# Reading spilled tiles back ahead of time: the first down chunk's forms, the last block's parts and the gate rows move from GpSimd's queue to the weights' queue

## The chip, the cores and the metric

One core of a Trainium2 chip runs the whole kernel. The metric is device time in microseconds (us) of one execution; 0.3% of it is 6.6 us. TensorE (PE) multiplies, VectorE (DVE) and ScalarE (ACT) do everything elementwise, GpSimd (POOL) and SyncE (SP) here only issue transfers: SP's queue loads weights, POOL's queue carries the traffic to and from scratch memory in DRAM.

## The reference, cut to what matters

```python
x = x + gate_m * rms_norm(o, g_post_mix)                  # the mixer's residual, 512 tokens x 2048
h = rms_norm(x, g_pre_ffn) * (1.0 + scale_f) + shift_f
f = (silu(h @ w_ffn_gate) * (h @ w_ffn_up)) @ w_ffn_down  # 2048 -> 5632 -> 2048
x = x + gate_f * rms_norm(f, g_post_ffn)                  # gate_f: a part of silu(c) @ w_ada + b_ada
```

Everything is float32. The kernel splits each operand into a rounded high part and the rest (hi, lo) and makes three matmuls of each product (`mm3`, L214 to L216).

## The kernel before, in words

**Up phase.** The 5632 FFN columns are cut into 22 blocks of 256 (`NBLK`). A block is worked in two halves `s` of the contraction. Of each half the gate and the up weights come as one load of 1 MB each (`raw_of`, L912) on SP's queue into four `wr` buffers. Seven products in the manner of Strassen (`q1`, `q2`, `q5`, `r7`, `r6`, `q4`, `r3`) replace eight; each takes sums of weights (`vadd`, L924), split by ACT (L906) and DVE (L907) into `wh` buffers, against a *form* of the activations (`a11`, `s1`, ...) that lies in SBUF. A half is 168 matmuls of 128x256.

**Spill.** All 128x512 tiles share one pool of 73 buffers (`t2`, tiles named `t`). After each pair of blocks, `pair_forms` makes the seven forms of the pair's result, and `spill_parts` stores hi and lo of each to DRAM (`gd`, L948, POOL's queue). The last pair (blocks 20, 21) stores no forms, only hi and lo of its four results (`gd[-1]`, eight tiles).

**Down phase.** Ten of the eleven pairs are consumed in five chunks `c_` of two pairs. A chunk makes, for each half `p` of the output columns, seven products of 24 matmuls of 128x512. At the first use of a form in a chunk, `back` (L1024) loads its four 256 KB tiles from DRAM on POOL's queue, 28 loads in a chunk. The down weights are loads of 1 MB on SP's queue (`w_fd`). ACT (L1042) copies a product to its accumulator in the first chunk, DVE adds it (L924) in the others; after the last chunk DVE combines the accumulators (L924, L838).

**Tail.** The last pair is multiplied plainly. `gate_rows(1, ...)` turns the column of FFN gates into four row tiles: two DVE operations on `ggcol`, a transpose by PE (L254), a copy by DVE (L256), a store to DRAM (`gg`, L257), and four loads that spread each quarter over 128 partitions (L260), the last two steps on POOL's queue. Eight `back` loads (`gl`) follow them there. Four loads of 1 MB (`w_fl`, SP's queue) are split into `t` tiles by ACT (L1082) and DVE (`minus`, L838). Then follow four token tiles times four column groups of 12 matmuls, each with an add (L1098), a square, a multiply by the gate row (L1101), and per token tile a norm, the residual (L1107) and the store of `y`.

The program's order on each engine follows the code; a scheduler moves instructions a little, and every buffer of a pool is waited for by whoever writes it next.

Of the kernel before, what the change touches and what calls it, by code (L numbers as in the profile page):

```python
# [11 lines left out]
F32 = mybir.dt.float32  # L12
F32R = mybir.dt.float32r
# [7 lines left out]
P = 128  # L21
# [8 lines left out]
NBLK = DFF // 256  # L30
# [47 lines left out]
def block_kernel(ctx, tc, x, c, pos, w_ada, cols, w_g1, w_kqvr, w_uq, w_uk, w_uv, wg17,  # L78
# [10 lines left out]
    dma = nc.sync.dma_start  # L89
    dma2 = nc.gpsimd.dma_start  # L90
# [3 lines left out]
    def nm(s):  # L94
        uid[0] += 1
        return f"{s}_{uid[0]}"
# [14 lines left out]
    def t2(dt=F32, n=512):  # L111
        return sp.tile([P, n], dt, tag="t2k", name=nm("t"))

    def bank(g):
        return pp.tile([P, 512], F32, tag="ps" + g, name=nm("ps"), bufs=4)

    def small(n, tag, bufs=8):
        return sm.tile([P, n], F32, tag=tag, name=nm(tag), bufs=bufs)
# [124 lines left out]
        V.tensor_tensor(out=scol[:, s], in0=scol[:, s], in1=g, op=ALU.mult)  # L243
        V.tensor_tensor(out=shcol[:, s], in0=adac[:, o + j0:o + j0 + n], in1=pc[:, o + j0:o + j0 + n], op=ALU.add)

    def gate_rows(i, rows):

        o = 48 * i + 32
        s = slice(16 * i, 16 * i + 16)
        gp = (C_GPOST, C_GPOSTF)[i]  # L250
        V.tensor_tensor(out=ggcol[:, s], in0=adac[:, o:o + 16], in1=pc[:, o:o + 16], op=ALU.add)
        V.tensor_tensor(out=ggcol[:, s], in0=ggcol[:, s], in1=pc[:, gp:gp + 16], op=ALU.mult)
        ps, rowd = bank("B"), dp.tile([16, P], F32, name=f"gg{i}")
        T.transpose(ps[:16, :P], ggcol[:, s], ident)  # L254
        r16 = t2(F32, P)
        V.tensor_copy(out=r16[:16, :], in_=ps[:16, :P])  # L256
        dma2(out=rowd, in_=r16[:16, :])  # L257
        flat = rowd.rearrange("a b -> (a b)").unsqueeze(0)
        for n in range(4):
            dma2(out=rows[n], in_=flat[:, n * 512:(n + 1) * 512].partition_broadcast(P))  # L260
        return rows


# [9 lines left out]
    v = small(NT, "v4", 1)  # L273
    V.tensor_reduce(out=v, in_=xs.rearrange("p (t n) -> p t n", n=4), axis=AX.X, op=ALU.add)
    v = rsqrt(v, D, NT)
# [135 lines left out]
    for which, src in ((0, ang), (1, al)):  # L411
# [4 lines left out]
        t = t2()  # L416
# [355 lines left out]
        pass  # L772
    chunks = fill_out()

    ggm = gate_rows(0, [t2() for _ in range(4)])
    with in_order():
        for slot in range(18):
            for g in range(4):
# [58 lines left out]
    def minus(out, a, b):  # L837
        V.tensor_tensor(out=out, in0=a, in1=b, op=ALU.subtract)  # L838
# [71 lines left out]
    def raw_of(src):  # L910
        raw = wp.tile([P, 2048], F32, tag="wr", name=nm("wr"))
        dma(out=raw, in_=src)  # L912
        return raw
# [9 lines left out]
    def vadd(out, a, b):  # L923
        V.tensor_tensor(out=out, in0=a, in1=b, op=ALU.add)  # L924
# [15 lines left out]
    advance(30)  # L940

    gd = []

    def spill_parts(src):
        made = []
        for v in parts(src):
            d = dp.tile([P, 512], F32, name=nm("gd"))
            dma2(out=d, in_=v.bitcast(F32))  # L948
            made.append(d)
        return made  # L950

    def pair_forms(g1, g2):

        (a11, a21), (a12, a22) = g1, g2
        made = {}
        made["a11"], made["a12"], made["a22"] = [spill_parts(v) for v in (a11, a12, a22)]
        minus(a22, a21, a22)
        made["s1"] = spill_parts(a22)
        minus(a21, a21, a11)
        made["s3"] = spill_parts(a21)  # L960
        minus(a11, a11, a22)
        made["s2"] = spill_parts(a11)
        minus(a12, a12, a11)
        made["s4"] = spill_parts(a12)
        return made

    g = []
    for j in range(NBLK):
        pss = {}
        for s in range(2):  # L970
            gr, ur = raw_of(w_fg[j, s]), raw_of(w_fu[j, s])
            b11, b21, b12, b22 = gr[:, :1024], gr[:, 1024:], ur[:, :1024], ur[:, 1024:]

            def product(name, f, src, tag):
                if s == 0:
                    pss[name] = bank(tag)
                up_product(pss[name], wparts(src), f, s, s == 0, s == 1)

            if j >= PRO:
                product("q1", "a11", b11, "A")  # L980
                if s == 1:
                    q1 = t2()
                    A.copy(out=q1, in_=pss["q1"])
                product("q2", "a12", b21, "A")
                if s == 1:
                    sg = t2()
                    vadd(sg, pss["q2"], q1)
                    A.activation(sg, sg, AF.Silu)
            else:
                q1, sg = early[j]  # L990
            vadd(b11, b11, b12)
            vadd(b12, b12, b22)
            product("q5", "s1", b11, "A")
            product("r7", "s3", b12, "A")
            vadd(b11, b11, b22)
            product("r6", "s2", b11, "B")
            if s == 1:
                w_, c22 = t2(), t2()
                minus(q1, pss["r6"], q1)
                vadd(w_, pss["r7"], q1)  # L1000
                vadd(q1, pss["q5"], q1)
                vadd(c22, pss["q5"], w_)
            vadd(b11, b11, b21)
            product("q4", "a22", b11, "B")
            if s == 1:
                minus(w_, pss["q4"], w_)
                A.activation(w_, w_, AF.Silu)
                V.tensor_tensor(out=c22, in0=c22, in1=w_, op=ALU.mult)
            product("r3", "s4", b22, "B")
            if s == 1:  # L1010
                vadd(q1, pss["r3"], q1)
                V.tensor_tensor(out=q1, in0=q1, in1=sg, op=ALU.mult)
        g.append((q1, c22))
        if len(g) == 2:
            if j < NBLK - 1:
                gd.append(pair_forms(*g))
            else:
                gd.append([[spill_parts(v) for v in blk] for blk in g])
            g = []


    def back(d):
        t = t2(F32R)
        dma2(out=t.bitcast(F32), in_=d)  # L1024
        return t

    acc = [[{} for _ in range(2)] for _ in range(2)]
    for c_ in range(NBLK // 4):
        fs = {}
        for p in range(2):  # L1030
            def product(name, f, src):
                if f not in fs:
                    fs[f] = [[back(d) for d in gd[2 * c_ + q][f]] for q in range(2)]
                w = [wparts(src[:, o:o + 1024]) for o in (0, 1024)]
                for tk in range(2):
                    ps = bank("AB"[tk])
                    for kk in range(4):
                        mm3(ps, cut(fs[f][kk // 2], (kk % 2) * 256 + tk * P, P), cut(w[kk // 2], (kk % 2) * 512, 512),
                            kk == 0, kk == 3)
                    if c_ == 0:  # L1040
                        a = acc[p][tk][name] = t2()
                        A.copy(out=a, in_=ps)  # L1042
                    else:
                        a = acc[p][tk][name]
                        vadd(a, ps, a)

            b11, b21 = raw_of(w_fd[c_, 0, 2 * p]), raw_of(w_fd[c_, 1, 2 * p])
            product("q1", "a11", b11)
            b22, b12 = raw_of(w_fd[c_, 1, 2 * p + 1]), raw_of(w_fd[c_, 0, 2 * p + 1])
            product("q2", "a12", b21)  # L1050
            vadd(b11, b11, b12)
            vadd(b12, b12, b22)
            product("r3", "s4", b22)
            product("q5", "s1", b11)
            product("r7", "s3", b12)
            vadd(b11, b11, b22)
            product("r6", "s2", b11)
            vadd(b11, b11, b21)
            product("q4", "a22", b11)
            if c_ == NBLK // 4 - 1:  # L1060
                for tk in range(2):
                    a = acc[p][tk]
                    vadd(a["q2"], a["q2"], a["q1"])
                    minus(a["r6"], a["r6"], a["q1"])
                    vadd(a["r7"], a["r7"], a["r6"])
                    vadd(a["r6"], a["r6"], a["q5"])
                    vadd(a["r6"], a["r6"], a["r3"])
                    vadd(a["q5"], a["q5"], a["r7"])
                    minus(a["q4"], a["q4"], a["r7"])
    facc = [[acc[n // 2][t % 2][("q2", "r6", "q4", "q5")[2 * (t // 2) + n % 2]] for n in range(4)] for t in range(NT)]  # L1070
    ggf = gate_rows(1, [t2() for _ in range(4)])


    gl = [[[back(d) for d in v] for v in blk] for blk in gd[-1]]
    wl = []
    for n in range(4):
        raw = raw_of(w_fl[n])
        row = []
        for k in range(4):
            hi, lo = t2(F32R), t2(F32R)  # L1080
            r = raw[:, k * 512:(k + 1) * 512]
            A.copy(out=hi, in_=r)  # L1082
            minus(lo, r, hi)
            row.append((hi, lo))
        wl.append(row)
    fsum = cp.tile([P, 4 * NT + 1], F32, name="fsum")
    for t in range(NT):
# [5 lines left out]
        for j, (n, o, w) in enumerate(parts_):  # L1093
# [3 lines left out]
            f = facc[t][n][:, o:o + w]  # L1097
# [4 lines left out]
        v = small(1, "v1")  # L1102
        V.tensor_reduce(out=v, in_=fsum[:, 4 * t:4 * t + len(parts_)], axis=AX.X, op=ALU.add)
        v = rsqrt(v, D)
        for n in range(4):
            f = facc[t][n]
# [58 lines left out]
```

## Time and the profile before

| what | value |
|---|---|
| median of 3 runs | 2198.98 us (2196.05 to 2203.56) |
| the profiled execution's own time | 2194.42 us |
| its span, from the first instruction to the last | 2192.6 us |
| mean granted TensorE clock in it | 0.977 |
| PE busy | 95% |
| DVE busy | 80% |
| ACT busy | 42% |
| POOL busy | 10% |

The table tells of shares over the whole span; the kernel has stages with different limits, so the rows below are taken from single places. The profiled execution took 1.8 us more than its span and 4.56 us less than the median of the runs.

### The profile page before, as it was taken

The numbers are of one execution on the slowest core, as the hardware profiler recorded it, in microseconds if no ns is written. First come the engines' busy times: TensorE is split into PE (matmuls) and PEld (weight loads), VectorE is DVE, ScalarE is ACT, GpSimd is POOL, SyncE is SP. The second block draws the span as 40 slices with busy tenths as digits, with TensorE's granted clock in tenths as the row PEclk, the third lists the DMA queues.
The fourth block names the chain that finished last, engine by engine and source line by source line (L and its number), as shares of the span: only waits on it lengthen the run. The fifth ranks groups of instructions, "written<-read, shape, count | busy, mean of one in ns | idle before, by whom it ended". The sixth has DMA issues, their size and how long they took to land. (4 is left out here: it accounts for less than half of the span.)

```text
span 2192.6 us, 31994 instructions
## 1 busy us (share of the span) xinstructions
PE 2078.5 (95%) x12714; PEld 1839.2 (84%) x12714; DVE 1754.2 (80%) x2236; ACT 919.3 (42%) x1277; POOL 227.7 (10%) x427
## 2 busy tenths in 40 slices
PE   6999999997999977999999999999999799999968
PEld 5888777774888766999999999999999688888856
DVE  6888987776476666889979889889888668889977
ACT  5433323334242676334444444444444353333332
POOL 0000000001211100011101101101100421121010
PEclk9999999998999987999999999999999899999989
DMA  8886786675574753345533434434434674664343
GB/s 333 317 318 237 279 316 230 254 266 207 189 255 159 265 195 116 152 185 190 198 132 145 183 116 152 176 125 166 152 127 172 240 308 148 232 228 168 115 155 134
DMA packets 83256, 440.55 MB, mean 201 GB/s; under 512 B 12296, under 2 KB 12408, under 8 KB 45473
## 3 DMA queue, kind: packets, MB, share of 16 engines
q1 hardware_dynamic: 49680, 329.67, 40.9%
q0 software_dynamic: 33424, 108.82, 13.2%
q8 instruction: 100, 1.64, 0.3%
q14 instruction: 50, 0.41, 0.1%
q10 hardware_dynamic: 2, 0.01, 0.0%
HBM read 379.19 MB, written 59.26 MB: 200 GB/s over the span
## 5 line engine op out<-in xcount | busy, mean ns | idle before, releaser
L214 PE MATMUL ps<-t,wh 128*128 128x256 f32 x2464 | 703.1, 285 | 20.2 <-DVE t L924 8.3
L906 ACT CAST wh<-wr 128x1024 fp32r<-128x1024 f32 x448 | 464.3, 1050 | 592.3 <-PE ps L215 328.0
L216 PE MATMUL ps<-t,wh 128*128 128x256 f32 x2464 | 700.9, 285 | 3.5 <-DVE wh L907 3.4
L215 PE MATMUL ps<-t,wh 128*128 128x256 f32 x2464 | 701.4, 285 | 0.0
L907 DVE TENSOR_TENSOR wh<-wr,wh 128x1024 fp32r<-128x1024 f32 x448 | 540.9, 1220 | 157.1 <-ACT wh L906 153.8
L214 PEld LDWEIGHTS ps<-t,wh 128*128 128x128 f32 x2464 | 477.4, 194 | 22.8 <-issue 8.4
L216 PEld LDWEIGHTS ps<-t,wh 128*128 128x128 f32 x2464 | 476.9, 194 | 4.2 <-DVE wh L907 4.1
L215 PEld LDWEIGHTS ps<-t,wh 128*128 128x128 f32 x2464 | 477.4, 194 | 0.0
L228 DVE CUSTOM_DVE_ANT_0 wr<-wr,cB 128x2048 f32<-128x2048 f32 x96 | 219.3, 2286 | 40.8 <-DMA wr<-w_ada 40.5
L214 PE MATMUL ps<-wh,t 128*128 128x512 f32 x560 | 218.5, 391 | 10.8 <-DMA t<-gd 10.8
L215 PE MATMUL ps<-wh,t 128*128 128x512 f32 x560 | 218.9, 391 | 2.9 <-DVE wh L907 2.9
L202 ACT CAST hi<-wr 128x1024 fp32r<-128x1024 f32 (+3 forms) x122 | 122.5, 1009 | 231.3 <-PE ps L215 145.0
L216 PE MATMUL ps<-wh,t 128*128 128x512 f32 x560 | 217.5, 390 | 1.8 <-DMA t<-gd 1.8
L924 DVE TENSOR_TENSOR wr<-wr,wr 128x1024 f32<-128x1024 f32 (+1 forms) x128 | 198.9, 1554 | 15.1 <-DMA wr<-w_fd 10.8
L203 DVE TENSOR_TENSOR lo<-wr,hi 128x1024 fp32r<-128x1024 f32 (+3 forms) x122 | 142.0, 1168 | 56.6 <-ACT hi L202 55.8
L214 PE MATMUL ps<-t,hi 128*128 128x512 f32 x432 | 169.0, 399 | 4.2 <-ACT t L300 2.9
L215 PE MATMUL ps<-t,hi 128*128 128x512 f32 x432 | 170.6, 395 | 2.4 <-DVE t L302 2.3
L216 PE MATMUL ps<-t,lo 128*128 128x512 f32 x432 | 169.2, 393 | 0.0
L948 POOL DMA_DIRECT2D gd<-t x148 | 80.0, 542 | 837.7 <-ACT t L833 785.9
L214 PE MATMUL ps<-hi,t 128*128 128x512 f32 x400 | 162.0, 405 | 3.3 <-ACT ps L888 2.4
L924 DVE TENSOR_TENSOR t<-ps,t 128x512 f32<-128x512 f32 x222 | 149.7, 683 | 9.2 <-issue 8.0
L215 PE MATMUL ps<-lo,t 128*128 128x512 f32 x400 | 157.1, 393 | 0.0
(229 smaller groups left out, 2520.0 us busy)
## 6 DMA issues: line engine op xcount, KB each, us to landing
wr<-w_ada SPq DMA_DIRECT2D x96, 1024.0 KB, 5.2
wr<-w_fg SPq DMA_DIRECT2D x56, 1024.0 KB, 4.8
wr<-w_fu SPq DMA_DIRECT2D x44, 1024.0 KB, 7.2
wr<-w_fd SPq DMA_DIRECT2D x40, 1024.0 KB, 5.8
gd<-t POOLq DMA_DIRECT2D x148, 256.0 KB, 2.6
t<-gd POOLq DMA_DIRECT2D x148, 256.0 KB, 4.8
wr<-w_kqvr SPq DMA_DIRECT2D x24, 1024.0 KB, 4.9
wr<-w_out SPq DMA_DIRECT2D x22, 1024.0 KB, 5.5
```

The costliest lines, as they stand in the source:

```text
L202: A.copy(out=hi[:, :n], in_=r)
L203: V.tensor_tensor(out=lo[:, :n], in0=r, in1=hi[:, :n], op=ALU.subtract)
L214: T.matmul(ps, lhsT=a, rhs=c_, start=start, stop=False)
L215: T.matmul(ps, lhsT=a, rhs=d_, start=False, stop=False)
L216: T.matmul(ps, lhsT=b, rhs=c_, start=False, stop=stop)
L228: V.tensor_tensor_reduce(out=raw, in0=raw, in1=cB, scale=1.0, scalar=0.0, op0=ALU.mult, op1=ALU.add, accum_out=adac[:, j:j + 1])
L906: A.copy(out=hi, in_=src)
L907: V.tensor_tensor(out=lo, in0=src, in1=hi, op=ALU.subtract)
L924: V.tensor_tensor(out=out, in0=a, in1=b, op=ALU.add)
L948: dma2(out=d, in_=v.bitcast(F32))
```

## The change

`gate_rows` is cut in two. `gate_out(i)` makes the gate column, transposes it and stores it; for the FFN it is called right before the loop over the blocks. `gate_rows(rowd, rows, issue)` makes the four loads, on the queue that it is given. `back` also gets the queue as an argument. The 28 loads of the first down chunk's forms are written at the end of the first half of the last block, on SP's queue. The eight loads of the last pair, the first two `w_fl` loads and the four gate loads are written in the last chunk, before the sixth of the seven products of its second half, on SP's queue too.

```diff
-    def gate_rows(i, rows):
+    def gate_out(i):
...
         dma2(out=rowd, in_=r16[:16, :])
+        return rowd
+
+    def gate_rows(rowd, rows, issue):
+
         flat = rowd.rearrange("a b -> (a b)").unsqueeze(0)
         for n in range(4):
-            dma2(out=rows[n], in_=flat[:, n * 512:(n + 1) * 512].partition_broadcast(P))
+            issue(out=rows[n], in_=flat[:, n * 512:(n + 1) * 512].partition_broadcast(P))
         return rows
...
     gd = []
+    gate_f = gate_out(1)
...
+    def back(d, issue):
+        t = t2(F32R)
+        issue(out=t.bitcast(F32), in_=d)
+        return t
+
+    def forms_back(c, f, issue):
+        return [[back(d, issue) for d in gd[2 * c + q][f]] for q in range(2)]
...
+            if j == NBLK - 1 and s == 0:
+                fs = {f: forms_back(0, f, dma) for f in ("a11", "a12", "s4", "s1", "s3", "s2", "a22")}
...
-        fs = {}
+        if c_ > 0:
+            fs = {}
...
-                    fs[f] = [[back(d) for d in gd[2 * c_ + q][f]] for q in range(2)]
+                    fs[f] = forms_back(c_, f, dma2)
...
+            if c_ == NBLK // 4 - 1 and p == 1:
+                gl = [[[back(d, dma) for d in v] for v in blk] for blk in gd[-1]]
+                wlr = [raw_of(w_fl[n]) for n in range(2)]
+                ggf = gate_rows(gate_f, [t2() for _ in range(4)], dma)
             product("r6", "s2", b11)
...
-    ggf = gate_rows(1, [t2() for _ in range(4)])
-
-
-    gl = [[[back(d) for d in v] for v in blk] for blk in gd[-1]]
+
+
...
-        raw = raw_of(w_fl[n])
+        raw = wlr[n] if n < 2 else raw_of(w_fl[n])
```

In the changed file `raw_of` stands at L916, `back` at L974, the spills at L953, the gate loads at L264, `minus` at L842, the split of weights at L910 and L911.

**SP's queue around the last block.** Before, the weights of its last half (`w_fg`, `w_fu`) are followed at once by the first down weights:

```order
L912 DMA wr_2617_15975<-w_fu 128x2048
L912 DMA wr_2639_16184<-w_fg 128x2048
L912 DMA wr_2640_16186<-w_fu 128x2048
L912 DMA wr_2675_16436<-w_fd 128x2048
L912 DMA wr_2676_16438<-w_fd 128x2048
L912 DMA wr_2689_16486<-w_fd 128x2048
```

Of the change, the same two weight loads come first, and then the form loads begin:

```order
L916 DMA wr_2669_16248<-w_fg 128x2048
L916 DMA wr_2670_16250<-w_fu 128x2048
L974 DMA t_2641_16192<-gd_1571_7672 128x512
L974 DMA t_2642_16194<-gd_1572_7674 128x512
L974 DMA t_2643_16196<-gd_1661_8356 128x512
L974 DMA t_2644_16198<-gd_1662_8358 128x512
L974 DMA t_2645_16200<-gd_1575_7680 128x512
```

They go on to 28, and the first down weights follow the last of them:

```order
L974 DMA t_2666_16242<-gd_1580_7690 128x512
L974 DMA t_2667_16244<-gd_1669_8372 128x512
L974 DMA t_2668_16246<-gd_1670_8374 128x512
L916 DMA wr_2705_16500<-w_fd 128x2048
L916 DMA wr_2706_16502<-w_fd 128x2048
L916 DMA wr_2715_16542<-w_fd 128x2048
```

So nothing moves ahead of the up weights, and every down weight now stands behind the 28 form loads, which POOL's queue issued before at their first use.

**The queues at the end.** Before, POOL's queue ends with the gate rows and the last pair's parts (`gd_2661_16408` and on are these), which stand behind the last chunk's form loads:

```order
L257 DMA gg1_19419<-t_3308_19421 16x128
L260 DMA t_3303_19412<-gg1_19419 128x512
L260 DMA t_3304_19413<-gg1_19419 128x512
L260 DMA t_3305_19414<-gg1_19419 128x512
L260 DMA t_3306_19415<-gg1_19419 128x512
L1024 DMA t_3309_19428<-gd_2661_16408 128x512
L1024 DMA t_3310_19430<-gd_2662_16410 128x512
```

Of the change, SP has the last part's load, the gate loads and then the last chunk's remaining down weights before the first `w_fl`:

```order
L974 DMA t_3300_19347<-gd_2704_16498 128x512
L264 DMA t_3303_19353<-gg1_7039 128x512
L264 DMA t_3304_19354<-gg1_7039 128x512
L264 DMA t_3305_19355<-gg1_7039 128x512
L264 DMA t_3306_19356<-gg1_7039 128x512
L916 DMA wr_3259_19142<-w_fd 128x2048
L916 DMA wr_3260_19144<-w_fd 128x2048
L916 DMA wr_3267_19182<-w_fd 128x2048
L916 DMA wr_3268_19184<-w_fd 128x2048
L916 DMA wr_3301_19349<-w_fl 128x2048
```

The other seven parts stand just ahead, among three of the four `w_fd` loads of the last chunk's first half. The store and the four gate loads are no longer next to each other: the store is issued before the first block.

**DVE at the end.** Before, these rows hold the end of the combinations (L924 and L838 with two `t`), the copy of the transposed gates and the first low parts of `w_fl` (L838 from a `wr`):

```order
L924 TENSOR_TENSOR t_2822_17046<-ps_3302_19384,t_2822_17046 128x512
L924 TENSOR_TENSOR t_2814_17007<-t_2814_17007,t_2790_16892 128x512
L924 TENSOR_TENSOR t_2798_16930<-t_2798_16930,t_2806_16968 128x512
L838 TENSOR_TENSOR t_2822_17046<-t_2822_17046,t_2806_16968 128x512
L256 COPY t_3308_19421<-ps_3307_19418 16x128
L838 TENSOR_TENSOR t_3319_19447<-wr_3317_19444,t_3318_19446 128x512
L838 TENSOR_TENSOR t_3321_19451<-wr_3317_19444,t_3320_19450 128x512
L838 TENSOR_TENSOR t_3323_19455<-wr_3317_19444,t_3322_19454 128x512
```

Of the change, one low part of `w_fl` stands earlier, among the combinations:

```order
L911 TENSOR_TENSOR wh_3314_19399<-wr_3259_19142,wh_3313_19398 128x1024
L911 TENSOR_TENSOR wh_3316_19403<-wr_3259_19142,wh_3315_19402 128x1024
L928 TENSOR_TENSOR t_2814_17000<-ps_3311_19369,t_2814_17000 128x512
L842 TENSOR_TENSOR t_3320_19449<-wr_3301_19349,t_3319_19448 128x512
L842 TENSOR_TENSOR t_2814_17000<-t_2814_17000,t_2772_16803 128x512
L928 TENSOR_TENSOR t_2816_17015<-ps_3312_19383,t_2816_17015 128x512
```

The other low parts follow the combinations as before, without the copy between:

```order
L842 TENSOR_TENSOR t_2824_17054<-t_2824_17054,t_2808_16976 128x512
L928 TENSOR_TENSOR t_2816_17015<-t_2816_17015,t_2792_16900 128x512
L928 TENSOR_TENSOR t_2800_16938<-t_2800_16938,t_2808_16976 128x512
L842 TENSOR_TENSOR t_3322_19453<-wr_3301_19349,t_3321_19452 128x512
L842 TENSOR_TENSOR t_3324_19457<-wr_3301_19349,t_3323_19456 128x512
L842 TENSOR_TENSOR t_3326_19461<-wr_3301_19349,t_3325_19460 128x512
L842 TENSOR_TENSOR t_3328_19465<-wr_3302_19351,t_3327_19464 128x512
```

The copy has moved to the start of the up phase, and the first low part of `w_fl` ahead of 15 combining operations.

## Rows read from the trace of the kernel before

**Rows 1.** The page, busy time of each engine.
```profile
PE 2078.5 (95%) x12714; PEld 1839.2 (84%) x12714; DVE 1754.2 (80%) x2236; ACT 919.3 (42%) x1277; POOL 227.7 (10%) x427
```
**Rows 2.** Waits of PE: engine, line, releaser: us in total, times, longest.
```profile
PE ps L214 <- DMA t<-gd: 29.0, 2, 18.2
```
**Rows 3.** Timeline of PE, from the up phase to the down phase.
```profile
1718.86 0.28 PE L215 MATMUL ps<-t,wh 128*128 128x256 f32 x1
1718.98 0.28 PE L216 MATMUL ps<-t,wh 128*128 128x256 f32 x1
1730.06 0.77 PE L214 MATMUL ps<-wh,t 128*128 128x512 f32 x1 [10.80 <-DMA t<-gd]
...
1733.51 0.80 PE L216 MATMUL ps<-wh,t 128*128 128x512 f32 x1 [1.83 <-DMA t<-gd]
```
**Rows 4.** Timeline of ACT, copies of the first products.
```profile
1740.71 0.57 ACT L1042 COPY t<-ps 128x512 f32<-128x512 f32 x1
...
1746.15 0.57 ACT L1042 COPY t<-ps 128x512 f32<-128x512 f32 x1
```
**Rows 5.** Windows: stretch, PE, PEld, DVE, ACT, POOL, PEclk, DMA share, GB/s.
```profile
1730.00:1735.00 5.00, 3.11 (x7) 2.04 (x8) 0.00 (x0) 0.00 (x0) 4.94 (x10) 0.50 0.87 273
...
1740.00:2119.00 379.00, 376.08 (x1657) 310.29 (x1655) 325.94 (x310) 163.39 (x178) 65.76 (x123) 1.00 0.54 200
```
**Rows 6.** Timeline of POOL at the same place.
```profile
1726.97 0.54 POOL L1024 DMA_DIRECT2D t<-gd  x1
...
1729.78 6.00 POOL L1024 DMA_DIRECT2D t<-gd  x11
```
**Rows 7.** Timeline of SP, the last up weights and the first down weights.
```profile
1671.29 0.33 SPq L912 DMA_DIRECT2D wr<-w_fu  x1
1690.62 19.76 SPq L912 DMA_DIRECT2D wr<-w_fd  x4
```
**Rows 8.** Windows as in rows 5: the x loads, and the last block.
```profile
5.00:10.00 5.00, 5.00 (x7) 1.66 (x5) 1.44 (x4) 4.83 (x13) 0.00 (x0) 1.00 0.96 344
...
1680.00:1690.00 10.00, 10.00 (x86) 10.00 (x85) 7.58 (x9) 3.40 (x4) 0.00 (x0) 1.00 0.01 2
```
**Rows 9.** DMA issues: times, KB each, us from issue to landing.
```profile
wr<-w_fd SPq DMA_DIRECT2D x40, 1024.0 KB, 5.8
```
**Rows 10.** Timelines of ACT and DVE, operations before the first down products.
```profile
1707.71 1.05 ACT L906 CAST wh<-wr 128x1024 fp32r<-128x1024 f32 x1 [0.51 <-PE ps L215]
...
1711.66 1.22 DVE L907 TENSOR_TENSOR wh<-wr,wh 128x1024 fp32r<-128x1024 f32 x1 [1.64 <-ACT wh L906]
...
1728.27 0.68 DVE L834 TENSOR_TENSOR t<-t,t 128x512 fp32r<-128x512 f32 x1
```
**Rows 11.** Timeline of PE, from the last chunk to the last matmul.
```profile
2118.75 0.27 PE L254 MATMUL ps<-cs,ggcol 128*16 128x128 f32 x1
2137.19 0.77 PE L214 MATMUL ps<-t,t 128*128 128x512 f32 x1 [18.17 <-DMA t<-gd]
...
2183.44 0.28 PE L216 MATMUL ps<-t,t 128*128 128x256 f32 x1
```
**Rows 12.** Timeline of POOL at the tail.
```profile
2122.33 0.51 POOL L257 DMA_DIRECT2D gg<-t  x1 [104.27 <-DVE t L256]
...
2136.94 0.54 POOL L1024 DMA_DIRECT2D t<-gd  x1 [0.38 <-issue]
```
**Rows 13.** Timeline of DVE at the tail.
```profile
2121.77 0.27 DVE L256 COPY t<-ps 16x128 f32<-16x128 f32 x1
2121.97 4.88 DVE L838 TENSOR_TENSOR t<-wr,t 128x512 fp32r<-128x512 f32 x8
```
**Rows 14.** Timelines of SP and ACT, the last pair's weights.
```profile
2098.09 14.06 SPq L912 DMA_DIRECT2D wr<-w_fl  x4
...
2110.26 8.53 ACT L1082 CAST t<-wr 128x512 fp32r<-128x512 f32 x16
```
**Rows 15.** Timeline of PE in the last chunk, a wait for DVE.
```profile
2091.87 0.50 PE L215 MATMUL ps<-wh,t 128*128 128x512 f32 x1 [1.95 <-DVE wh L907]
```

More of the change, by code (lines that the diff above doesn't have):

```diff
@@ L773, in block_kernel @@
     chunks = fill_out()
-    ggm = gate_rows(0, [t2() for _ in range(4)])
+    ggm = gate_rows(gate_out(0), [t2() for _ in range(4)], dma2)
     with in_order():
@@ L1019, in block_kernel @@
             g = []
[L1022 to L1025, printed above, removed]
     acc = [[{} for _ in range(2)] for _ in range(2)]
     for c_ in range(NBLK // 4):
-        fs = {}
+        if c_ > 0:
+            fs = {}
         for p in range(2):
```

## The prediction

> **What bounds the kernel now.** I read the page's busy times first: PE is busy 2078.5 us [rows 1], so a gain must come from PE's idle time, and the question is which of it the change touches. PE's waits answer that: 29.0 us in two waits end with the landing of a tile from DRAM [rows 2]. The timeline of PE shows both places. At the start of the down phase PE's last up matmul starts at 1718.98 and the first down matmul at 1730.06, and 1.83 us more are lost at 1733.51, to the same cause [rows 3]. At the tail PE is through at about 2118.7 and goes on at 2137.19 [rows 11].
>
> The gaps cost more than their length, since the matmuls behind them are slow: in 1730 to 1735 the granted clock is 0.50 (1.2 GHz), whereas over the 379 us of down chunks it is 1.00 and a matmul takes 376.08/1657 = 0.227 us [rows 5]. So I measure each place from the end of the work before it to a point where PE runs fully again.
>
> First place: the first product's second copy on ACT starts at 1740.71, and the next product's 5.44 us later [rows 4], which is 24 x 0.227, the undisturbed pace. Without a gap the first product would run from 1719.1 and be copied at about 1719.1 + 5.44 + 0.2 = 1724.7. The place costs 1740.7 - 1724.7 = **16.0 us**. The cause is seen at POOL: its first form loads are issued at 1726.97 and 1729.78, behind the last spills in the same queue [rows 6].
>
> Second place: POOL stores the gate row at 2122.33, and the last part's load is only issued at 2136.94, behind the gate loads [rows 12]. PE then works from 2137.19 to 2183.44 [rows 11] without a stop: 16 groups of 12 matmuls are 192 x 0.227 = 43.6 us, and some 12 of them at half clock (the first takes 0.77, as the first one did at 1730.06) add 12 x 0.2 = 2.4. So the tail is PE's own from 2137 on, and whatever starts it earlier is passed on to the end.
>
> **The change, part by part. Form loads on SP's queue: -15.7 us.** The order shows them behind the last up weights, issued at 1671.29, and ahead of the down weights, which before went out from 1690.62, when their buffers came free [rows 7]. Two questions decide: do the forms land before 1719, and do the down weights still?
>
> A form load needs a free buffer. By the order, 13 of the 28 wait only for stores of long ago; the other 15 wait for tiles that the first half of the last block reads last in its first four products. A half is 168 matmuls, 0.12 apart [rows 3], or 20.2 us; so that half runs from 1678.8 to 1699.0, and four sevenths of it end at 1690.4. The transfer engines have room: in 1680 to 1690 they move 2 GB/s, and the 256 KB loads of x on the same queue ran at 344 GB/s [rows 8]. At that rate the two up weights (2.1 MB) are in by 1677.4, 13 forms (3.4 MB) by 1687.3, and the other 15 (3.9 MB, 11.4 us) between 1698.7 and 1690.4 + 11.4 = 1701.8. All lie before 1719.
>
> The first down weight (1.05 MB) then lands between 1701.8 and 1705, with the 5.8 us from issue to landing of such loads [rows 9] inside that. Its cast ran at 1707.71, its low part was through at 1712.9 [rows 10], and PE wants it at 1719.1; so it may land as late as 1707.7 + 6.2 = 1713.9. Up to there 10.5 MB have to pass from 1671.3 on, in 42.6 us: the rate must stay above 246 GB/s. The lowest rate of a stretch full of form loads is 273 (1730 to 1735, at a share of 0.87 and from POOL's queue [rows 5]); by that the weight lands at 1709.8. I take no delay from it.
>
> What is late next is DVE: it works on spilled parts until 1728.95 [rows 10], and the low parts of the third product's weights, 1.22 each, follow at 1730.1 and 1731.4. PE reaches that product at 1719.1 + 2 x 5.44 = 1730.0 and its second half of weights at 1731.4. I take 0.3 us of stall, bounded by 0 and 1.2 (one split). That makes -16.0 + 0.3.
>
> **POOL's queue without 28 loads: 0.** The next chunks' loads start earlier. PE is busy 376.08 of the 379 us of the chunks [rows 5], so at most 2.9 are to be had; nothing shows a loss.
>
> **Gate column early: +0.5.** A transpose of 0.27 on PE [rows 11], a copy of 0.27 on DVE [rows 13] and a store of 0.51 on POOL [rows 12] move to the start of the up phase. Between nothing (hidden) and 1.05 (all on the path); I take the middle.
>
> **Parts, gate rows and two last weights on SP's queue: -18.2.** The weights `w_fl` went out from 2098.09 before [rows 14] and do so still. With the parts there, PE goes on at 2118.75. What it lacks then is DVE: the first low part of `w_fl` now stands among the combinations, so PE has 8 matmuls (1.8 us, to 2120.6), and the second one comes behind the combinations. Those ended at 2121.77, and a low part takes 4.88/8 = 0.61 [rows 13]; with one ahead they end at 2122.4, and the second low part at 2123.0. **New stall: 2.4 us.** From there both engines are nearly even for the first token tile and the first group of the second: PE has 52 matmuls, 11.8 us, to 2134.8; DVE has 15 low parts, 3 adds and 3 multiplies, 21 x 0.61 = 12.8, to 2135.2. The other 11 groups are 132 x 0.227 = 30.0 us of PE, to 2165.2, against 2183.44 + 0.1 before. ACT's 16 casts took 8.53 us from 2110.26 [rows 14] and stay ahead. Bounds: without the stall -20.8; with DVE fully in front of PE for the first four groups (16 low parts, 4 adds, 4 multiplies, and four squares' waits of some 0.6) -14.
>
> **Sum:** -15.7 + 0.5 - 18.2 = -33.4. The profiled execution of 2194.42 us would become 2161.0. It lies 4.56 below the median of the runs, 2198.98, so the predicted time is 2198.98 - 33.4 = **2165.6**.
>
> **The rivals.** *Down weights late behind the forms.* For it: they now stand in the same queue behind 7.3 MB. If the buffers of all 28 loads came free only with the end of the half, 1699.0, the forms would be in at 1720.3, the weight at 1723.4, 9.5 us behind 1713.9: 2175.1. Against it: 13 loads need no such buffer. The Trainium skill's page "DMA: Bandwidth & Descriptors", section "Queues, rings and completion order", says that SP owns one row of rings, each consumed in order, while rings of different rows are served in turn. By that rule the down weight gets no share before the forms have passed, which it would from POOL's queue; no row of this trace shows two kinds of load on SP competing.
>
> *The tail's clock or DVE.* PE stood 1.95 us at 2091.87 [rows 15] and stayed at clock 1.00 behind it, but was at 0.50 behind the gap of 10.8 [rows 3, 5]. If it falls in the new stall, some 12 matmuls take 0.2 more each, +2.4: 2168.0; with DVE in front as bounded above, +4.2: 2169.8. The Trainium skill's "TensorE: Matmul & The Clock Gate", section "HAM oscillation — how this bites in real kernels", warns that a loop that pauses again and again for data keeps falling back to the lower rate. By that rule the even stretch of 2123 to 2135, where PE waits for one low part after another, would be the danger, not the one stall; the short waits of this trace's down phase do not bear it out, as the clock of 1.00 shows [rows 5].
>
> *One prefetch does nothing*, because its loads wait for buffers that come free no earlier than the use: the other remains, 2198.98 - 15.7 or - 18.2, so 2181 to 2183. The order speaks against it.
>
> *Slower: SP's queue blocked in the last chunks.* The twelve 256 KB loads stand among the last chunk's down weights. If one waits for a buffer that only comes free at the end of a chunk's half (7 x 5.44 = 38 us), each down weight behind it waits too, and PE with it. It decides from 33.4 us of waiting on; at 38 it is +5: 2204. Against it: such a buffer comes free with every product, 5.44 us apart, and four of them.
>
> **How the numbers follow.** Forecast 0.70; tail's clock or DVE 0.12; down weights late 0.08; one prefetch idle 0.03; gain lost in a queue up to no change 0.03; slower 0.04. The forecast's own range is 2161 to 2169. Low end: no stall (-2.4 more) and runs that stand to the median as the profiled one does (-4.6): 2158. High end: weights late, 2175.1, and the 2.9 between the lowest and the middle run: 2178. What can be told from no change is 0.3%, 6.6 us: faster by more 0.93, within 0.03, slower 0.04.
>
> **What would show it.** In the changed profile: no wait of PE for a form tile; 28 form loads on SP between 1671 and 1692; the first product's second copy near 1724.7; clock 1.00 across 1720 to 1740; PE's tail from about 2103 (15.7 earlier) with a wait for DVE of 2 to 3 us, and its last matmul near 2150. Wrong would make it: a wait of PE or ACT for `w_fd` after 1700, a half clock in the tail, or SP standing on one of the twelve loads.

## The result and the profile after

The changed kernel took 2160.75 us (median of 4 runs, 2159.18 to 2170.64) against 2201.27 (median of 4, 2196.05 to 2203.66). The ratio is 0.9837, with a 95% interval of 0.982 to 0.9855: 1.6% faster, some 36 us; the two medians alone lie 40.5 apart. The forecast was 2165.6, in a range of 2158 to 2178.

The profiled execution is the longest of the four: 2170.64 us, span 2168.9. Its up phase ends 8.7 us later than before (1727.69 in place of 1718.98 [rows 3]), and that is no work of the change: the lag has grown to 7 us by 340 us and 12 by 540 us, and is back at 9 by 785 us, in the mixer, whose code is the same. Over the fourteen profiles of this study the end of the up phase lies between 1714.8 and 1728.5. So the places are read by two distances that leave the mixer out: **D1** from the start of the last up matmul to that of the last matmul of the chunks, **D2** from there to the end of the span. Before, D1 is 2118.52 - 1718.98 = 399.54 and D2 is 2192.6 - 2118.52 = 74.08.

PE's timeline of the changed kernel, at the first place:

```profile
1727.69 0.28 PE L216 MATMUL ps<-t,wh 128*128 128x256 f32 x1
1727.81 0.40 PE L214 MATMUL ps<-wh,t 128*128 128x512 f32 x1
```

The down phase follows the up phase by one matmul's spacing, where [rows 3] had 10.80 and 1.83 of waiting. Its waits from 1670 us to the end (releaser, sum, times, longest):

```profile
PE ps L215 <- DVE wh L911: 3.0, 2, 2.0
PE ps L215 <- DVE t L842: 2.0, 1, 2.0
```

No wait for a tile from DRAM is left [rows 2]; the first line stood before too, the second is new. The queue that issues the loads (SP), and windows (PE, PEld, DVE, ACT, POOL, PEclk, DMA share, GB/s):

```profile
1680.01 0.33 SPq L916 DMA_DIRECT2D wr<-w_fu  x1
1680.64 20.12 SPq L974 DMA_DIRECT2D t<-gd  x28
1701.05 309.64 SPq L916 DMA_DIRECT2D wr<-w_fd  x33
```
```profile
1685.00:1690.00 5.00, 5.00 (x44) 5.00 (x43) 5.00 (x7) 2.47 (x3) 0.00 (x0) 1.00 1.03 399
...
1730.00:1735.00 5.00, 5.00 (x24) 4.14 (x23) 5.00 (x7) 3.07 (x5) 2.15 (x4) 1.00 0.50 202
```

The 28 loads are out by 1700.8, 27 us before PE's first down matmul, while the transfer engines move 399 GB/s in all; the clock is 1.00 where it was 0.50 [rows 5]. D1 is 2112.00 - 1727.69 = **384.31**.

The second place, on PE and on DVE:

```profile
2112.00 0.39 PE L216 MATMUL ps<-wh,t 128*128 128x512 f32 x1
2112.23 0.39 PE L214 MATMUL ps<-t,t 128*128 128x512 f32 x1
...
2116.18 0.50 PE L215 MATMUL ps<-t,t 128*128 128x512 f32 x1 [1.98 <-DVE t L842]
...
2118.50 0.63 PE L214 MATMUL ps<-t,t 128*128 128x512 f32 x1
...
2159.67 0.28 PE L216 MATMUL ps<-t,t 128*128 128x256 f32 x1
```
```profile
2114.24 1.29 DVE L928 TENSOR_TENSOR t<-t,t 128x512 f32<-128x512 f32 x2
2115.44 3.09 DVE L842 TENSOR_TENSOR t<-wr,t 128x512 fp32r<-128x512 f32 x5
```

The tail begins at once (18.17 us of waiting before [rows 11]), makes 8 matmuls, and stands 1.98 us for the second low part of the last weights, which DVE starts behind the combinations, at 2115.44. From 2117.7 on some eight matmuls come 0.43 apart, at half clock, as the window there shows:

```profile
2118.00:2120.00 2.00, 2.00 (x6) 1.54 (x5) 1.79 (x4) 0.53 (x1) 0.00 (x0) 0.50 0.76 221
```

D2 is 2168.9 - 2112.00 = **56.90**.

So from the end of the up phase on, 32.4 us are gone: 15.2 in D1 and 17.2 in D2.

### The profile page after: what moved, and what is told of

It reads as the page before. It is cut to its first block, busy times and chain, and to the rows that moved or that the text cites. A ratio compares the mean times of both kernels' runs of the same rounds, so it can differ in the third digit from the quotient of the medians.

```text
span 2168.9 us, 31978 instructions
## 1 busy us (share of the span) xinstructions
PE 2081.8 (96%) x12714; PEld 1841.0 (85%) x12714; DVE 1752.8 (81%) x2236; ACT 918.8 (42%) x1277; POOL 206.0 (9%) x387
## 4 chain that ended last, share of the span: by engine, by line
PE 70%; issue 15%; DVE 8%; DMA 5%; ACT 1%; POOL 1%; SPq 0%; DVEq 0%; ACTq 0%; POOLq 0%
PE ps L214 22%; PE ps L215 22%; PE ps L216 22%; DMA wr<-w_ada 3%; DVE wr L228 2%; DVE t L928 1%; DMA wr<-w_kqvr 1%; DVE wh L911 1%; DVE lo L203 1%; PE ps L584 1%; PE ps L611 1%; DVE wr L928 1%; PE ps L583 1%; DMA t<-x 0%; DMA wr<-w_uq 0%
## 5 line engine op out<-in xcount | busy, mean ns | idle before, releaser
L910 ACT CAST wh<-wr 128x1024 fp32r<-128x1024 f32 x448 | 464.7, 1051 | 592.8 <-PE ps L215 335.1
L911 DVE TENSOR_TENSOR wh<-wr,wh 128x1024 fp32r<-128x1024 f32 x448 | 540.7, 1220 | 141.1 <-ACT wh L910 138.2
L214 PE MATMUL ps<-hi,t 128*128 128x512 f32 x400 | 161.6, 404 | 1.2 <-DVE t L209 0.9
L216 PE MATMUL ps<-hi,t 128*128 128x512 f32 x400 | 156.2, 393 | 0.0
```

The lines of the kernel that those rows point to most:

```text
L214: T.matmul(ps, lhsT=a, rhs=c_, start=start, stop=False)
L216: T.matmul(ps, lhsT=b, rhs=c_, start=False, stop=stop)
L910: A.copy(out=hi, in_=src)
L911: V.tensor_tensor(out=lo, in0=src, in1=hi, op=ALU.subtract)
```

## The experiments

All distances in us, from each run's profile; ratios to the kernel before, which ran beside each of them. The diffs are against the changed kernel where nothing else is said.

| kernel | D1 | D2 | ratio, 95% interval |
|---|---|---|---|
| before | 399.54 | 74.08 | |
| the change | 384.31 | 56.90 | 0.9837 (0.9820 to 0.9855) |
| forms only | 384.33 | 72.98 | 0.9918 (0.9886 to 0.9950) |
| tail only | 399.64 | 55.04 | 0.9912 (0.9880 to 0.9944) |
| gate column early only | 403.54 | 55.25 | 0.9939 (0.9908 to 0.9969) |
| parts ahead of gate rows only | 401.96 | 59.56 | 0.9924 (0.9897 to 0.9952) |
| forms by POOL's queue | 384.33 | 55.00 | 0.9856 (0.9838 to 0.9874) |
| two forms ahead | 389.24 | 55.08 | one run |
| forms three times, SP | 423.59 | 55.24 | one run |
| forms three times, POOL | 393.17 | 55.22 | one run |
| the change again | 384.35 | 55.26 | 0.9829 (0.9806 to 0.9852) |
| all by POOL's queue | 386.32 | 55.31 | 0.9833 (0.9813 to 0.9853) |
| combinations late | 385.87 | 53.04 | 0.9809 (0.9791 to 0.9827) |
| and half of them on POOL | 385.09 | 54.84 | 0.9826 (0.9804 to 0.9848) |

**Are the two places independent?** First the forms alone (the gate column, the gate rows and the parts as before the change), then the tail's part alone:

```diff
-    gate_f = gate_out(1)
...
-            if c_ == NBLK // 4 - 1 and p == 1:
-                gl = [[[back(d, dma) for d in v] for v in blk] for blk in gd[-1]]
-                wlr = [raw_of(w_fl[n]) for n in range(2)]
-                ggf = gate_rows(gate_f, [t2() for _ in range(4)], dma)
...
+    ggf = gate_rows(gate_out(1), [t2() for _ in range(4)], dma2)
+    gl = [[[back(d, dma2) for d in v] for v in blk] for blk in gd[-1]]
...
-        raw = wlr[n] if n < 2 else raw_of(w_fl[n])
+        raw = raw_of(w_fl[n])
```

> Only the 28 form loads go to SP's queue at the last block; gate column, gate rows and the last pair's parts stay as before the change. Two distances are read, which leave the mixer's own scatter out: D1 from the last up matmul to the last matmul of the down chunks (399.5 us before, 384.3 after), D2 from there to the end of the span (74.1 before, 56.9 after). Theory A, the two places are independent: D1 384.3 +-0.5, D2 74.1 +-0.7, ratio to the kernel before 0.993. Rival B, one place pays for the other (what is gained at the first is lost again in a later wait that the second edit hides): D1 above 388 or D2 above 76.

```diff
-            if j == NBLK - 1 and s == 0:
-                fs = {f: forms_back(0, f, dma) for f in ("a11", "a12", "s4", "s1", "s3", "s2", "a22")}
...
-        if c_ > 0:
-            fs = {}
+        fs = {}
```

> Only the tail's part of the change: gate column early, parts, gate rows and two last weights on SP's queue in the last chunk; the first chunk's forms come from POOL's queue at their first use. Theory A: D1 399.5 +-0.7, D2 56.9 +-0.7, ratio 0.992. Rival B: D1 above 401 (twelve more loads ahead of down weights in SP's queue cost PE something), or D2 above 60.

PE's waits for a tile from DRAM in the first, and in the second:

```profile
PE ps L214 <- DMA t<-gd: 17.2, 1, 17.2
```
```profile
PE ps L214 <- DMA t<-gd: 10.9, 1, 10.9
...
PE ps L216 <- DMA t<-gd: 1.8, 1, 1.8
```

Each takes away its own wait and leaves the other: D1 384.33 with the forms, D2 55.04 with the tail. Theory A held; D2 of the first is 1.1 shorter than the kernel before's, since its wait is 1 us shorter (17.23, was 18.17), a little beyond the 0.7 allowed. D2 of the second is 1.2 below its band too: the 56.9 expected there was that of the changed kernel's first profile, half clock included, and here the clock stayed at 1.00.

**Was it the queue or the store in front?** Only the gate column moves; the twelve loads stay on POOL's queue, the gate rows ahead (against the kernel before):

```diff
+    gate_f = gate_out(1)
...
-    ggf = gate_rows(1, [t2() for _ in range(4)])
+    ggf = gate_rows(gate_f, [t2() for _ in range(4)], dma2)
```

> Only the gate column is made and stored before the first block; gate rows and the last pair's parts stay on POOL's queue, at the end, with the gate rows ahead. Theory A, it is the order in POOL's queue and not the queue that held the parts back (they stood behind a store that could only be made when PE and DVE were through): with the store gone, the twelve loads wait only for free buffers, come 28 loads after the last chunk's first ones, and land before PE needs them: D2 57 to 60, D1 399.5. Rival B, POOL's queue is too slow or too full for them: D2 65 to 74.

In the other, the gate column stays at the end, and the parts' loads are written ahead of it (against the kernel before):

```diff
-    ggf = gate_rows(1, [t2() for _ in range(4)])
     gl = [[[back(d) for d in v] for v in blk] for blk in gd[-1]]
+    ggf = gate_rows(1, [t2() for _ in range(4)])
```

> The kernel before with one thing changed: the eight loads of the last pair's parts are written ahead of the gate rows. The gate column is still made at the end. Theory A: the parts land before PE needs them and the gate rows are needed only by DVE's multiply, about 10 us behind the first tail matmul; PE loses only its transpose: D2 57 to 60. Rival B, the gate chain itself holds the tail (store 1.6, loads 6.1 and more, and the accumulators wait for it): D2 64 to 70.

POOL's timeline of the first, its last rows, and then PE's of the second at the tail:

```profile
2031.31 1.07 POOL L974 DMA_DIRECT2D t<-gd  x2 [3.01 <-PE ps L216]
2032.67 0.54 POOL L974 DMA_DIRECT2D t<-gd  x1 [0.29 <-PE ps L216]
```
```profile
2118.09 0.47 PE L214 MATMUL ps<-t,t 128*128 128x512 f32 x1
2122.01 0.80 PE L215 MATMUL ps<-t,t 128*128 128x512 f32 x1 [3.44 <-DVE t L838]
```

With the store gone, POOL has issued its last load at 2033, 87 us before PE's first tail matmul (2120.18): D2 is 55.25, as with the whole tail's part (55.04) and below the 57 to 60 expected. With the parts ahead it is 59.56; PE waits 3.44 for DVE, which has no low part ahead of the combinations here, and half clock follows. In both the parts came in time, so the 18 us were the place behind one store in a queue, and neither POOL's queue nor the gate chain itself. D1, expected as before, grew by 4.0 and 2.4 in these two. Half clock in the last chunk (below) makes some 1.6 of it in each. In the second the other 0.8 is more half clock at the first place, where eleven matmuls behind PE's second wait come slowly in place of six. In the first, longer waits for DVE in the last chunk make 0.9, the first place 0.3, and the third chunk 1.1, where a down weight comes late to DVE (it waits 3.0 at most for one before):

```profile
1886.15 2.29 DVE L928 TENSOR_TENSOR wr<-wr,wr 128x2048 f32<-128x2048 f32 x1 [4.45 <-DMA wr<-w_fd]
```

Why that weight is late stays open; the twelve loads are issued only from 2021 us on.

**The same for the forms.** The 28 loads at the same place on POOL's queue:

```diff
-                fs = {f: forms_back(0, f, dma) for f in ("a11", "a12", "s4", "s1", "s3", "s2", "a22")}
+                fs = {f: forms_back(0, f, dma2) for f in ("a11", "a12", "s4", "s1", "s3", "s2", "a22")}
```

> The changed kernel with the 28 form loads written at the same place but on POOL's queue, the rest as changed. D1 is the distance from the last up matmul to the last matmul of the down chunks (399.5 us before, 384.3 after). Theory A, what counts is when the loads are issued and not on which queue: D1 384.3 +-0.7, and no wait of PE for a tile from DRAM. Rival B, SP's queue is needed (POOL's starts them later, or its last spills, behind the 28 loads, come late and hold the tiles that the down phase wants): D1 387 or more.

D1 is 384.33, and no wait for a tile is left: the queue does not matter. With the parts on POOL's queue too, and the gate column early, no load of the change is on SP's:

> No load moves to SP's queue: the 28 form loads are written at the last block, as in the change, but on POOL's queue; the gate column is stored early; gate rows and the last pair's parts stay at the end of the code, on POOL's queue. Theory A, the whole gain is that loads are issued earlier: D1 384.3 +-0.5, D2 55.0 to 56.9, ratio to the changed kernel 1.000. Rival B, SP's queue has a part in it: D1 or D2 longer by 1 us and more.

D2 is 55.31, the ratio 0.9833 beside 0.9829 of the changed kernel in the same runs. D1 is 2.0 longer, at waits for DVE in the last chunk of 1.79 and 1.54 (0.97 and 1.98 in the changed kernel's second profile), which make 0.4, and at half clock behind one of them, which makes 1.6 and comes by chance (below). By the distance as it stands rival B would have D1; without the half clock it lies in theory A's band, and by the runs nothing is told apart. A longer first wait there stands in both kernels that have an early store and the twelve loads on POOL's queue (2.25 and 1.79); its cause stays open.

**How many forms are needed ahead.** `forms_back(0, f, dma)` for `a11` and `a12` alone, the others at their first use:

> The changed kernel with only the first two forms (8 loads) fetched ahead on SP's queue; the other 20 loads are issued by POOL at their first use, behind the last spills. Theory A, the gap is that of the first forms' landing: PE reaches the third product 10.9 us behind the last up matmul, about when the fourth load of the kernel before had nearly landed (its two waits ended 11 and 14.5 us behind it): a wait of 1 to 4 us there and no half clock, D1 386 to 389. Rival B, every form that is not ahead costs its own wait: waits for DRAM at several products, 7 us and more in sum and the clock at half, D1 392 to 398.

```profile
1739.31 0.47 PE L214 MATMUL ps<-wh,t 128*128 128x512 f32 x1 [3.04 <-DMA t<-gd]
```

One wait of 3.04 us, 14.2 us behind the last up matmul (1725.08), as theory A had it; half clock in the last chunk adds 1.6. D1 is 389.24, 0.2 above its bound. Eight loads of 28 bring two thirds of the first place's gain.

**What the loads ahead may cost.** All 28 loads repeated twice into the same tiles, on SP's queue as shown, and in a second kernel on POOL's (`dma2`):

```diff
+                for _ in range(2):
+                    for f in fs:
+                        for q in range(2):
+                            for d, t in zip(gd[q][f], fs[f][q]):
+                                dma(out=t.bitcast(F32), in_=d)
```

> The changed kernel, and behind the 28 form loads on SP's queue all of them twice more, into the same tiles (56 loads, 14.7 MB, more). Theory A, one queue is worked in order, so the down weights wait for the whole of it: at the 400 GB/s of the changed kernel's form loads the first down weight comes about 37 us later, 18 to 20 us too late; with some half clock D1 403 to 410. Rival B, loads of one queue share the engines, or the weights have slack enough: D1 384 to 388.

> As the run before, but the 56 repeated loads are on POOL's queue; the first 28 stay on SP's. The same bytes move at the same time. Theory A, the cost of many loads ahead is their place in SP's queue: D1 384 to 387. Rival B, it is the bytes: D1 as in the run with them on SP's queue, 403 to 410.

SP's queue and PE in the first, then in the second:

```profile
1699.06 48.94 SPq L1032 DMA_DIRECT2D t<-gd  x56
1749.52 43.82 SPq L916 DMA_DIRECT2D wr<-w_fd  x8
```
```profile
1759.93 1.22 PE L214 MATMUL ps<-wh,t 128*128 128x512 f32 x2 [34.28 <-ACT wh L910]
```
```profile
1703.79 92.87 SPq L916 DMA_DIRECT2D wr<-w_fd  x12
```
```profile
1726.44 0.79 PE L216 MATMUL ps<-wh,t 128*128 128x512 f32 x1 [6.18 <-DMA t<-gd]
```

On SP the first down weight is issued at 1749.52, 24.2 us behind the last up matmul (1725.37), where the changed kernel has it 26.6 ahead of it: 50.8 later. PE stands 34.3 for its cast. D1 is 423.59, slower than before by 24 us: the direction is theory A's, the size was too small by 14 to 21 us, of which 12 are the 56 loads, which took 48.9 us and not 37. On POOL the down weights go out 15.7 us ahead of the last up matmul, and PE waits for none of them. It waits 6.2 us for a tile that is still being written for the third time, a wait that the repetition itself makes; so D1 (393.17) fits neither number, but who is waited for does tell the two apart. The Trainium skill's "DMA: Bandwidth & Descriptors", section "Queues, rings and completion order", has SP's loads on one row of rings that is worked in order; the trace agrees in effect (0 us of waiting for weights with the repeats in the other queue, 34.3 with them in front), though what it shows is that SP issues the weight late, before any ring has it.

The first run also gives the change's own margin, which the forecast had put at some 9 to 12 us: 50.8 us of delay made PE 34.4 late, so by an estimate the down weights could have gone out 16.4 us later without a loss.

**What is left at the tail.** The changed kernel again, and with DVE's low parts of the first two last weights ahead of the second half's combinations:

> The changed kernel once more, so that the next three are compared with it in the same runs. D1 384.3 +-0.3 from the last up matmul to the last matmul of the chunks. D2 from there to the end: 55.1 with the clock at 1.00 behind the stall of 2.0 us (seen in five of the six other profiles with this tail), 56.9 with the half clock (seen in the first profile of this kernel). Theory A, the half clock behind a stall of this length comes in some executions only: either number is possible, and the same program gives both. Rival B, it belongs to this program: 56.9 again.

```diff
-            if c_ == NBLK // 4 - 1:
-                for tk in range(2):
...
+            if c_ == NBLK // 4 - 1 and p == 0:
+                combine(0)
...
+    wl = [split_last(n) for n in range(2)]
+    combine(1)
...
+    wl += [split_last(n) for n in range(2, 4)]
```

> The changed kernel with DVE's low parts of the first two last weights written ahead of the combinations of the second half, which are needed only by the third column group. Theory A, PE's stall of 2.0 us at the tail is the order on DVE: the stall goes, and with it the chance of the half clock: D2 52.8 to 53.4, D1 384.3 +-0.5, ratio to the changed kernel 0.9985. Rival B, DVE is the bound of the tail's first groups and the stall only moves: D2 54.5 or more, or the low parts delay the last product's and D1 grows by 0.6 and more.

The same stall in the changed kernel's second profile, and its window:

```profile
2106.32 0.50 PE L215 MATMUL ps<-t,t 128*128 128x512 f32 x1 [1.98 <-DVE t L842]
2106.66 0.39 PE L216 MATMUL ps<-t,t 128*128 128x512 f32 x1
```
```profile
2105.00:2110.00 5.00, 3.68 (x16) 3.06 (x17) 5.00 (x10) 0.69 (x2) 0.00 (x0) 1.00 0.25 75
```

The clock stays at 1.00 here and D2 is 55.26: theory A, the half clock is the execution's and not the program's. (All six other profiles with this stall at the tail have 1.00 too, not five of them.) With the combinations late the tail's stall is gone and D2 is 53.04, as expected. Half clock behind the last chunk's own stall makes D1 385.87 in this profile. The ratio of 0.9809 is the best of all, but 0.002 under the changed kernel's in the same runs, with intervals that overlap: better by the distance, not told apart by the runs.

Last, the first half's 14 combinations on POOL (against the run before this one):

```diff
-                combine(0)
+                combine(0, nc.gpsimd)
```

> As the run before, and the 14 combinations of the first half are done by POOL, which is idle there, in place of DVE. They stand among DVE's work where PE waits 1.0 and 2.0 us for low parts in the last chunk. Theory A: these waits go, D1 381.2 to 381.8, D2 as in the run before. Rival B, POOL's additions slow DVE's or come too late for the first adds of the tail: D1 384 or more, or D2 longer by 1 us and more.

The operations of its combining line (ns: least, median, most), and one of DVE's low parts beside them:

```profile
L1044 POOL TENSOR_TENSOR t<-t,t x14: 1292/2236/3233, 2031.1 to 2076.4; 128x512 f32<-128x512 f32 x14
L1044 DVE TENSOR_TENSOR t<-t,t x14: 678/679/1776, 2072.0 to 2109.1; 128x512 f32<-128x512 f32 x14
```
```profile
2054.13 1.71 DVE L911 TENSOR_TENSOR wh<-wr,wh 128x1024 fp32r<-128x1024 f32 x1
```

Rival B: an addition takes POOL 2.24 us in place of DVE's 0.68, and DVE's low part beside it takes 1.71 in place of 1.22. Ten low parts of 128x1024 lie for more than half of their time beside an addition of POOL: one took 1.21, seven 1.63 to 1.72, two 2.3; the 126 of the down chunks and the tail that lie beside none took 1.21 to 1.23. Eight of DVE's additions with one input in PSUM (128x512) lie beside POOL's in the same way and kept their 0.68. PE still waits 1.86 us in the last chunk, and several times for less. D1 is 385.09, and D2 54.84.

## Why the prediction was right

*Form loads ahead, -15.7:* measured -15.2. The mechanism is that of the text: loads out early, no wait, no half clock. Three readings in it were off. The cost of the place before was read from ACT's copy at 1740.71 [rows 4], but that copy stood behind a cast that began at 1739.75 with 1.06. PE itself starts the second product 20.80 us behind the last up matmul before, and 5.59 behind it after the change (first line before, second line after):

```profile
1739.78 0.39 PE L214 MATMUL ps<-wh,t 128*128 128x512 f32 x1
```
```profile
1733.28 0.39 PE L214 MATMUL ps<-wh,t 128*128 128x512 f32 x1
```

So the place cost 15.2, not 16.0, and all of it is gone. And the stall of 0.3 at the third product is not there: PE's waits show none. The third reading is that of the down weights' margin, 16.4 by the estimate above. The cast at 1707.71 [rows 10], which the text gives to the first down weight, is of an up weight: with the repeats on SP's queue it runs at its old place, 11.3 us ahead of the last up matmul, when no down weight has been issued. The down weight's cast, which the low part at 1711.66 waits for, is the next one:

```profile
1710.58 1.05 ACT L906 CAST wh<-wr 128x1024 fp32r<-128x1024 f32 x1 [1.82 <-PE ps L215]
```

That moves the latest landing by 2.9 us, from 1713.9 to 1716.8. And the weight landed earlier than forecast: issued at 1701.05 with 6.8 us to landing, it was there 19.8 us ahead of the last up matmul, where the text had 14.0 to 17.2; the transfer engines moved 399 GB/s and not 344 [rows 8].

*POOL's queue without 28 loads, 0, and the gate column early, +0.5:* D1 is as without the first term. The second was not there either. PE stood 0.28 us for ACT at this place before; the transpose runs in that time. The matmul behind it comes 9.04 us later than before, which is the mixer's lag alone, as the matmuls ahead of the transpose come as much later (first line before, the others after):

```profile
834.06 0.39 PE L214 MATMUL ps<-t,wh 128*128 128x256 f32 x1 [0.28 <-ACT wh L906]
```
```profile
842.66 0.27 PE L254 MATMUL ps<-cs,ggcol 128*16 128x128 f32 x1
843.10 0.38 PE L214 MATMUL ps<-t,wh 128*128 128x256 f32 x1 [0.17 <-ACT wh L910]
```

*The tail, -18.2:* measured -17.2 in the first profile and -18.8 in the second. The stall of 2.4 was forecast from DVE's order and came as 1.98 of waiting. The difference of 1.6 between the two profiles is the half clock, the first of the tail's rivals, which was priced at 2.4 and given part of 0.12. In nine profiles with this stall it came once. The rule of the Trainium skill's "TensorE: Matmul & The Clock Gate", section "HAM oscillation — how this bites in real kernels", that repeated pauses keep the array slow, is not tested here: between 2123 and the end PE pauses no more.

*The sum:* -33.4 forecast; the distances give -32.4 and, in the second profile, 399.54 + 74.08 - 384.35 - 55.26 = -34.0. That it comes so near is in part luck: the first place was read 0.8 too dear, and the 0.3 and 0.5 set against it for a stall and for the gate column did not come, so that the three errors cancel. The two measurements by runs give 0.9837 and 0.9829, some 36 and 38 us, with intervals that hold 33.4. The rest between them and the distances is not explained beyond the mixer's scatter.

*The rivals:* weights late behind the forms is real as a mechanism, but by the estimate above needs 16 us more of loads; the twelve loads on SP's queue held nothing up (D1 399.64 with the tail alone). What the prediction left out is that the queue was beside the point: it costed the move to SP's queue as one thing, and did not see that the early store alone frees the twelve loads where they stood.

## What to carry to other kernels

A load that waits behind a late store in a queue costs as much as a slow one: look first at what stands ahead of it, since moving that one store brought the second place's whole gain (D2 55.25, beside 55.04 with the loads on another queue too), and moving the loads to another queue nothing more. What fetching ahead needs is free buffers at that time and room until the next load in the queue is wanted; measure that room by repeating the loads. When two long waits fall, the next one is an order on the engine that fed them, here DVE's, with 2 us.

## What the runs showed of the hardware

The same stall can leave the clock alone or halve it. In eleven profiles, of ten kernels, PE waits 1.93 to 1.98 us for DVE at the same place of the last chunk; in seven of them the clock stayed at 1.00, in four the next six to eight matmuls came 0.43 apart, at 1.2 GHz, which costs about 1.6 us. At the tail's stall of 1.98 it is one in nine, and there two profiles of one and the same program differ.

An addition of 128x512 on POOL took 1.29 to 3.23 us, and while POOL added, most of DVE's subtractions of 128x1024, which have both inputs in SBUF, took some 1.7 in place of 1.22, 40% longer. DVE's additions of 128x512 with one input in PSUM kept 0.68 beside POOL.
